# Smaller constant tables, a load plan by row length, pooling moved ahead of the attention pairs, and rotary tables moved into the MLP

## The chip, the cores and the metric

The kernel runs on one core of a Trainium2 chip. The metric is the device time of one execution in microseconds, the median of several runs. An engine is named as in the profile: PE (TensorE, matmuls), PEld (its weight loads), DVE (VectorE), ACT (ScalarE), POOL (GpSimd), SP (SyncE, which here issues all transfers that count).

## The reference

Two transformer blocks on 256 tokens of width 1024, in float32. Cut to what matters:

```python
def first_block(x, ...):
    h = rms_norm(x, g_mix_pre)
    u, q, k, v = split(h @ w_in)                     # 512 columns each
    y_pool = pool_mixer(u, w_pool, pool_scale)       # trailing means of 2, 4, 8, 16 tokens, per group
    y_attn = moba_attention(q, k, v, rel_bias)       # 8 heads, causal softmax with a position bias
    x = x + rms_norm(concatenate([y_pool, y_attn]) @ w_out, g_mix_post)
    x = x + rms_norm(conv_ffn(rms_norm(x, g_ffn_pre), w_up, conv_w, conv_b, w_down), g_ffn_post)
    return x + (p @ w_ple) * sigmoid(x @ w_ple_gate)

def second_block(x, mem, positions, ...):
    for i in range(2):                               # i = 0: sparse attention, i = 1: latent attention
        proj = x @ w_in[i]
        mix = nsa_mixer(proj, ...) if i == 0 else mla_mixer(proj, ...)   # both use rotary tables
        xa = memory_cross_attention(xq, mk, mv)      # mk, mv = mem @ mem_w_kv[i]
        x = layer_norm(ALPHA * x + concatenate([mix, xa]) @ w_out[i])
        x = layer_norm(ALPHA * x + hier_moe(x, ...)) # 16 experts, 2 per token, 3 matrices of 2 MB each
```

The rotary tables are cosines and sines of `positions` times fixed frequencies. The two sets of experts are 2 x 16 x 3 x 2 MB = 201 MB of the 293 MB that the kernel reads.

## The kernel before, in words

The kernel does not issue instructions as its functions are called. Each call is recorded as an operation (`Plan.record`), with what it reads and writes. At the end `Plan.order` goes through all operations as a list scheduler: for every engine it knows a modelled time at which the engine is free, and a model of each operation's duration (`Plan.cost`), and it places next the operation that can start first, in order of rank among those that can start about equally early. The rank is the place in the program; operations recorded inside `nc.filler()` get a rank behind everything, so they are taken only where an engine has nothing else to do, until something with an earlier rank needs them. The instructions are then emitted in this order. On the chip each engine takes its own instructions strictly in that order, and waits on semaphores; a modelled time decides nothing there but the order.

The model of a transfer: its issue takes 0.06 us of SP, and then all transfers share one modelled wire with 2.6e-6 us per byte. SP is not planned further than 3 us ahead of the wire.

Tiles are placed by the same scheduler: `arena` (208 units of 256 floats per partition, 1 KB each) for all working tiles, `tiny` (64 slots of 16 floats) for scalars per token such as means and inverse roots, and eight PSUM banks. A tile far ahead of the rest of the program may only be placed when enough room stays free; this is what stops loads that run ahead. A chunk of an expert's matrix is 256 x 512 floats, 512 KB, four arena units. Weights are float32; for the attention and MLP matrices they are split into a high and a low part on ACT, DVE and POOL (`split`, `put_split`: the cast to the high part, then a subtraction), and each product is three matmuls (`mm3`). Expert matrices are used in float32 as they are.

The order of the stages: `setup`, `block1` (projections `feat` and `tok512` of q, k, v; four pairs of heads, `pair(j)`, each with two query tiles, a softmax in `attend`, transposes and the product with v; then the projection of u and four `pool_mix(g)`; then the output projection, rows 512 to 1023 first: `order = [4, 5, 6, 7, 0, 1, 2, 3]`), the memory's keys and values for both layers (`memory`, as filler), the norms and transposes of the residual, `mlp` (eleven blocks of 256 hidden features, with `rope_tables` as filler at its start), `nsa`, `moe(0)`, `mla`, `moe(1)`, `finish`. Constant tables stay in SBUF the whole time: `ones` (128 x 128 floats), `busy` (128 x 512 bf16, the operand of dummy matmuls that PE runs in long gaps), `tiny`.

`row_bcast`, `rows_bcast` bring gains and biases of the norms to all partitions; `rows_bcast` picks a row by a matmul with a column `pick`, made anew for every row by one addition. `ln_gained` is the norm behind an expert stage; it writes into the tile `self.x`, whose old contents were last read at the fourth pair of experts (`pr == 3` in `moe`).

## Time and profile before

| | us |
|---|---|
| median of 3 runs | 1069.38 |
| lowest and highest | 1068.79, 1071.5 |
| the profiled execution | 1069.15 |
| its span, first to last instruction | 1067.5 |
| outside the span | 1.65 |

The granted clock of PE is 0.989 of full speed over the span. The page's first part gives the busy time of each engine. A stage's limit is not read from these shares but from windows cut at the stages, below. In a window row the columns are: the stretch, its length, then for PE, PEld, DVE, ACT and POOL the busy time with the number of instructions, then PE's granted clock, the mean busy share of the transfer engines, and GB/s.

### The profile page before, as it was taken

How to read it: one execution, taken by the hardware profiler on the slowest of the kernel's cores; microseconds unless marked ns; L12 is line 12 of the kernel's file. 1: busy time of each engine (PE TensorE's matmuls, PEld its weight loads, DVE VectorE, ACT ScalarE, POOL GpSimd, SP SyncE). 2: the span in 40 equal slices, each digit the busy share in tenths (PEclk: the TensorE clock that was granted, in tenths of full speed). 3: DMA queues.
4: the chain of work that ended last, by engine and by line, in shares of the span. 5: the costliest groups of instructions: out<-in, count | busy, mean ns of one | idle time of the engine just before them, and what ended most of it. 6: DMA issues, size and time to landing. Idle time of an engine off the chain costs nothing. (4 is left out here: it accounts for less than half of the span.)

```text
span 1067.5 us, 16507 instructions
## 1 busy us (share of the span) xinstructions
PE 1022.5 (96%) x6119; PEld 692.8 (65%) x6125; DVE 598.6 (56%) x1533; ACT 424.1 (40%) x973; POOL 78.7 (7%) x83
## 2 busy tenths in 40 slices
PE   8989899999999999999999899999999999999994
PEld 6878799999988888877444343435887434443431
DVE  6599999777767799996241111107996523111104
ACT  3475774343435456674231111107664422111103
POOL 0223200000002000310200000001100000000000
PEclk9999999999999999999999999999999999999998
DMA  8995115745576622387899999999669699999994
GB/s 304 360 307 200 58 44 195 242 155 184 210 271 198 217 100 79 100 311 261 281 382 386 385 369 377 382 387 375 245 228 322 229 360 386 386 387 387 387 387 151
DMA packets 172359, 292.85 MB, mean 274 GB/s; under 512 B 9251, under 2 KB 59340, under 8 KB 172268
## 3 DMA queue, kind: packets, MB, share of 16 engines
q1 hardware_dynamic: 172268, 291.69, 77.3%
q8 instruction: 51, 0.84, 0.3%
q14 instruction: 40, 0.33, 0.1%
HBM read 290.60 MB, written 1.06 MB: 273 GB/s over the span
## 5 line engine op out<-in xcount | busy, mean ns | idle before, releaser
L641 PE MATMUL ps<-span,span 128*128 128x256 f32 (+5 forms) x5464 | 954.2, 397 | 10.0 <-DVE span L641 7.0
L641 PEld LDWEIGHTS ps<-span,span 128*128 128x128 f32 (+3 forms) x5464 | 630.0, 173 | 304.4 <-issue 223.2
L641 DVE TENSOR_TENSOR span<-span,span 128x512 fp32r<-128x512 f32 (+7 forms) x425 | 256.7, 645 | 18.1 <-ACT span L641 15.4
L641 ACT CAST span<-span 128x512 fp32r<-128x512 f32 (+7 forms) x343 | 182.1, 581 | 55.2 <-DVE span L641 16.9
L641 DVE TENSOR_TENSOR span<-ps,span 128x512 fp32r<-128x512 f32 (+3 forms) x104 | 56.6, 549 | 149.5 <-ACT span L641 98.7
L641 DVE SCALAR_TENSOR_TENSOR span<-span,tiny,ps 128x512 f32<-128x512 f32 x16 | 12.0, 748 | 202.6 <-PE ps L641 191.3
L641 POOL TENSOR_TENSOR span<-span,span 128x512 fp32r<-128x512 f32 (+3 forms) x43 | 60.6, 1422 | 734.0 <-ACT span L641 443.9
L641 ACT CAST span<-ps 128x512 fp32r<-128x512 f32 (+1 forms) x63 | 32.3, 518 | 155.8 <-PE ps L641 145.4
L641 ACT COPY span<-ps 128x512 f32<-128x512 f32 (+1 forms) x106 | 50.8, 497 | 93.6 <-PE ps L641 87.1
L641 PE MATMUL ps<-cst,span 128*128 128x128 f32 (+1 forms) x363 | 59.5, 284 | 19.0 <-DVE span L641 12.4
L641 ACT ACTIVATE span<-ps 128x512 f32<-128x512 f32 (+3 forms) x33 | 18.5, 559 | 118.9 <-PE ps L641 113.2
L641 PEld LDWEIGHTS ps<-cst,span 128*128 128x128 f32 (+1 forms) x363 | 40.7, 142 | 36.2 <-DVE span L641 13.1
L641 ACT ACTIVATE span<-ps,tiny 128x256 f32<-128x256 f32 (+3 forms) x96 | 44.5, 473 | 21.5 <-DVE tiny L641 13.9
L641 ACT ACTIVATE span<-ps,vecs 128x256 f32<-128x256 f32 (+2 forms) x52 | 25.6, 524 | 67.3 <-PE ps L641 67.2
L641 ACT ACTIVATE span<-span 128x256 f32<-128x256 f32 (+4 forms) x36 | 16.1, 450 | 86.9 <-DVE span L641 86.5
L641 ACT ACTIVATE span<-span,tiny 128x256 f32<-128x256 f32 (+3 forms) x63 | 31.7, 525 | 11.9 <-DVE tiny L641 11.6
L641 DVE TENSOR_REDUCE tiny<-ps 64x1 f32<-64x2 f32 (+3 forms) x78 | 29.8, 391 | 9.2 <-PE ps L641 7.2
L641 DVE TENSOR_SCALAR span<-ps,vecs 128x256 f32<-128x256 f32 (+2 forms) x35 | 16.6, 491 | 29.4 <-ACT span L641 27.9
L641 DVE CAST span<-span 128x512 fp32r<-128x512 f32 (+6 forms) x76 | 28.5, 382 | 2.7 <-DMA span<-in_w_in_dram 1.8
L641 DVE SCALAR_TENSOR_TENSOR span<-span,vecs,span 128x255 f32<-128x255 f32 (+2 forms) x52 | 25.4, 498 | 0.8
L979 PE MATMUL ps<-busy 128*128 128x512 bf16 x88 | 23.3, 411 | 1.8 <-POOL busy L975 1.4
L641 DVE TENSOR_SCALAR span<-span,tiny 128x256 f32<-128x256 f32 (+2 forms) x73 | 22.7, 338 | 0.2
(107 smaller groups left out, 345.3 us busy)
## 6 DMA issues: line engine op xcount, KB each, us to landing
span<-in_moe_w_gate_dram SPq DMA_DIRECT2D x128, 512.0 KB, 8.9
span<-in_moe_w_up_dram SPq DMA_DIRECT2D x128, 512.0 KB, 9.2
span<-in_moe_w_down_dram SPq DMA_DIRECT2D x128, 512.0 KB, 8.7
span<-in_w_up_dram SPq DMA_DIRECT2D x22, 1024.0 KB, 5.3
span<-in_w_out_dram SPq DMA_DIRECT2D x12, 1024.0 KB, 10.5
span<-in_w_down_dram SPq DMA_DIRECT2D x11, 1024.0 KB, 5.0
span<-in_w_in_dram SPq DMA_DIRECT2D x7, 1024.0 KB, 13.0
span<-in_nsa_w_in_dram SPq DMA_DIRECT2D x7, 1024.0 KB, 9.9
```

Source lines behind the costliest of these rows:

```text
L641: getattr(eng, op)(*[real(x) for x in a], **{n: real(x) for n, x in k.items()})
L979: return lambda: nc.nc.tensor.matmul(nc.banks[bank], busy[:, :128], busy, start=True, stop=True)
```

## The change

Six things are changed together.

1. Tables that stay: `tiny` goes from 64 slots to 12 (and the free slots that far-ahead work must leave, from 12 to 4), `ones` from 128 columns to one that is read with stride zero, `busy` from 512 columns to 128 read four times. The arena goes from 208 to 212 units.
2. The plan's model of loads: an issue costs 0.47 us of SP instead of 0.06; a byte costs 2.584e-6 us where a row of the source is 2 KB or more, 2.8e-6 from 1 KB, 3.4e-6 below, and 4.6e-6 for what goes over the wire in the first 8 us.
3. In `block1` the projection of u and the load of `w_pool` come ahead of the pairs, `pool_mix(j)` comes ahead of `pair(j)`, and the output projection takes its rows in order.
4. `rope_tables` is recorded at the fifth block of the MLP (`c == 4`), still as filler, and may not start before the last operation recorded until then.
5. `ln_gained` writes into a new tile for x.
6. The columns `pick` are made once for all rows in the setup, and the rounded identity `identr` once in the setup instead of once in each `moe`.

```diff
-    FAR = {"ps": 2, "ws": 5, "row": 0, "tiny": 12}
+    FAR = {"ps": 2, "ws": 5, "row": 0, "tiny": 4}
...
-            return 1.0 if eng == "POOL" else 0.06
+            return 1.0 if eng == "POOL" else 0.47
...
+    @staticmethod
+    def pace(src, at):
+
+        step, n = src.ap[-1]
+        run = 4 * n if step == 1 else 4
+        return 4.6e-6 if at < 8.0 else 2.584e-6 if run >= 2048 else 2.8e-6 if run >= 1024 else 3.4e-6
...
-                wire = max(wire, end + 1.3) + o.bytes * 2.6e-6
+                wire = max(wire, end + 1.4)
+                wire += o.bytes * self.pace(calls[0][2][1], wire)
...
-ARENA = 208
-TINY = 64
+ARENA = 212
+TINY = 12
...
-            t, pick = nc.tile([D], F32, "row"), self.sml([1], F32R)
-            nc.vector.tensor_add(pick, self.ident[:, row:row + 1], self.ident[:, 32 + row:33 + row])
+            t, pick = nc.tile([D], F32, "row"), self.picks[:, row:row + 1]
...
-        self.ones = self.stay([128, 128], "ones")
+        self.ones = self.stay([128, 1], "ones")
...
-        busy = self.keep.tile([128, 512], BF, name="busy")
+        busy = self.keep.tile([128, 128], BF, name="busy")
...
+        self.identr, self.picks = self.stay([128, 128], "identr", F32R), self.stay([128, 8], "picks", F32R)
+        nc.scalar.copy(self.identr, self.ident)
+        nc.vector.tensor_add(self.picks, self.ident[:, 0:8], self.ident[:, 32:40])
...
         mixT = self.hilo()
+        self.feat(W, 0, 512, h, mul(u))
+        self.wp = self.mid([4, 128])
+        nc.sync.dma_start(self.wp, A["w_pool"].rearrange("g c d -> c g d"))
...
         for j in range(4):
+            self.pool_mix(j, u, mixT)
             pair(j)
-        self.feat(W, 0, 512, h, mul(u))
-        self.wp = self.mid([4, 128])
-        nc.sync.dma_start(self.wp, A["w_pool"].rearrange("g c d -> c g d"))
-        for g in range(4):
-            self.pool_mix(g, u, mixT)
...
-        order = [4, 5, 6, 7, 0, 1, 2, 3]
+        order = [0, 1, 2, 3, 4, 5, 6, 7]
...
-        with nc.filler():
-            self.rope_tables()
         Y = [[self.ps() for t in range(2)] for n in range(2)]
...
         for c in range(11):
+            if c == 4:
+                with nc.filler():
+                    nc.after = nc.ops[-1]
+                    self.rope_tables()
+                    nc.after = None
...
-        nc, x = self.nc, self.x
+        nc = self.nc
+        x = self.x = self.big([2, D])
...
-                idr = self.sml([128], F32R)
-                self.copy(idr, self.ident)
...
-                        self.returned(F[t][n], idr, z[0], z[1], False, False)
+                        self.returned(F[t][n], self.identr, z[0], z[1], False, False)
```

`finish` and `mla` read `self.x` instead of the name `x` that they took before; matmuls that used `ones` use it with stride zero.

## Rows read from the trace of the kernel before

**Rows 1.** The page: busy time of PE, share of the span, instructions.

```profile
PE 1022.5 (96%) x6119; PEld 692.8 (65%) x6125; DVE 598.6 (56%) x1533; ACT 424.1 (40%) x973; POOL 78.7 (7%) x83
```

**Rows 2.** Windows cut at the stages; columns as told above.

```profile
40.00:57.00 17.00, 16.21 (x134) 15.38 (x133) 5.82 (x12) 3.71 (x7) 6.31 (x5) 1.00 1.06 369
...
73.00:91.00 18.00, 18.00 (x98) 15.01 (x97) 17.98 (x42) 12.93 (x26) 3.77 (x10) 1.00 0.52 176
91.00:105.00 14.00, 14.00 (x79) 12.29 (x78) 14.00 (x30) 6.74 (x17) 7.27 (x4) 1.00 0.86 293
105.00:131.00 26.00, 19.83 (x144) 18.36 (x144) 24.75 (x85) 16.83 (x38) 6.44 (x5) 0.93 0.21 66
131.00:318.00 187.00, 187.00 (x1306) 175.71 (x1306) 148.43 (x317) 86.18 (x174) 2.63 (x2) 1.00 0.55 185
...
360.00:521.00 161.00, 155.36 (x1159) 126.39 (x1161) 136.25 (x454) 93.28 (x262) 16.93 (x20) 0.99 0.53 183
521.00:727.00 206.00, 200.48 (x942) 81.61 (x938) 33.56 (x63) 32.53 (x59) 3.43 (x4) 0.99 1.04 379
...
757.00:840.00 83.00, 79.53 (x539) 64.61 (x540) 70.92 (x199) 50.60 (x138) 6.61 (x5) 1.00 0.64 224
840.00:1050.00 210.00, 207.67 (x984) 83.84 (x980) 35.70 (x69) 35.25 (x63) 4.40 (x4) 1.00 1.04 378
```

**Rows 3.** Groups of PE, 131 to 318 us: shapes, count, busy us, mean ns, idle before.

```profile
L641 PE MATMUL ps<-span,span 128*128 128x256 f32 x1020 | 124.2, 283 | 0.0
L641 PE MATMUL ps<-span,span 128*128 128x512 f32 x284 | 66.5, 390 | 0.0
```

**Rows 4.** Timeline at 56 us: start, us, instruction, idle before and who ended it.

```profile
56.67 0.62 ACT L641 CAST span<-span 128x512 fp32r<-128x512 f32 x1 [12.32 <-DMA span<-in_memT_dram]
...
59.19 0.54 PE L641 MATMUL ps<-cst,span 128*128 128x128 f32 x2 [2.98 <-ACT span L641]
```

**Rows 5.** Timeline of PE, 105 to 131 us.

```profile
109.16 1.12 PE L641 MATMUL ps<-cst,span 128*128 128x128 f32 x4 [3.72 <-DVE span L641]
109.92 2.67 PE L641 MATMUL ps<-span,span 128*128 128x256 f32 x12
...
120.23 1.67 PE L641 MATMUL ps<-span,span 128*128 128x256 f32 x12
...
130.85 0.38 PE L641 MATMUL ps<-cst,r 128*128 128x128 f32 x1 [1.17 <-DVE r L641]
```

**Rows 6.** Groups of DVE by shape, 101.5 to 131 us.

```profile
L641 DVE SCALAR_TENSOR_TENSOR tiny<-tiny 128x1 f32<-128x1 f32 x24 | 7.3, 316 | 0.0
...
L641 DVE TENSOR_SCALAR span<-span 128x256 f32<-128x256 f32 x6 | 2.8, 463 | 0.0
L641 DVE SCALAR_TENSOR_TENSOR span<-span,span 128x256 f32<-128x256 f32 x4 | 2.7, 670 | 0.0
...
L641 DVE SCALAR_TENSOR_TENSOR span<-span 128x256 f32<-128x256 f32 x2 | 0.8, 418 | 0.0
```

**Rows 7.** Timeline of ACT, 126 to 140 us: table loads.

```profile
127.27 1.28 ACT L986 ACT_TABLE_LOAD   x1
128.56 0.20 ACT L986 ACTIVATE dump<-zero 128x1 f32<-128x1 f32 x1
...
135.31 1.28 ACT L986 ACT_TABLE_LOAD   x1
```

**Rows 8.** An issue in SP's timeline; two windows of 20 us for their GB/s.

```profile
4.71 0.47 SPq L641 DMA_DIRECT2D span<-in_w_in_dram  x1
...
20.00:40.00 20.00, 20.00 (x111) 16.42 (x110) 16.92 (x59) 12.24 (x23) 1.30 (x1) 1.00 1.09 356
...
560.00:580.00 20.00, 20.00 (x108) 9.13 (x106) 2.95 (x9) 3.12 (x6) 0.00 (x0) 1.00 1.05 386
```

**Rows 9.** The chain that ended last: start, us, what.

```profile
1021.18 10.79 DMA span<-in_moe_w_up_dram
```

**Rows 10.** Groups of DVE by shape, 20 to 24 us: the picks.

```profile
L641 DVE TENSOR_TENSOR span<-cst 128x1 fp32r<-128x1 f32 x8 | 1.1, 152 | 0.0
```

More of the change, by code (lines that the diff above doesn't have):

```diff
@@ L973, in setup @@
             nc.gpsimd.memset(self.eps[:, i:i + 1], e)
-        busy = self.keep.tile([128, 512], BF, name="busy")
+        busy = self.keep.tile([128, 128], BF, name="busy")
         nc.nc.gpsimd.memset(busy, 0.0)
         def idle(bank):
-            return lambda: nc.nc.tensor.matmul(nc.banks[bank], busy[:, :128], busy, start=True, stop=True)
+            return lambda: nc.nc.tensor.matmul(nc.banks[bank], busy, busy.unsqueeze(1).to_broadcast([128, 4, 128]), start=True, stop=True)
         nc.idle = idle
@@ L998, in setup2 @@
         nc.gpsimd.memset(self.ones, 1.0)
-        for t, s in ((self.identb, self.ident), (self.causalb, causal), (self.befb, before), (self.onesb, self.ones)):
+        self.identr, self.picks = self.stay([128, 128], "identr", F32R), self.stay([128, 8], "picks", F32R)
+        nc.scalar.copy(self.identr, self.ident)
+        nc.vector.tensor_add(self.picks, self.ident[:, 0:8], self.ident[:, 32:40])
+        for t, s in ((self.identb, self.ident), (self.causalb, causal), (self.befb, before), (self.onesb, self.ones.to_broadcast([128, 128]))):
             nc.vector.tensor_copy(t, s)
@@ L1014, in routers @@
             p = self.ps()
-            nc.tensor.matmul(p[:, :40], self.ones, s.rearrange("p a n -> p (a n)"), start=True, stop=True)
+            nc.tensor.matmul(p[:, :40], self.ones.to_broadcast([128, 128]), s.rearrange("p a n -> p (a n)"), start=True, stop=True)
             nc.vector.tensor_add(self.rb[:, l], self.rb[:, l], p[:, :20])
@@ L1853, in finish @@
     def finish(self, F, rows, out):
-        x = self.x
         def done(t, n):
             ns = slice(n * 512, n * 512 + 512)
-            self.nc.sync.dma_start(out[t * 128:t * 128 + 128, ns], x[:, t, ns])
+            self.nc.sync.dma_start(out[t * 128:t * 128 + 128, ns], self.x[:, t, ns])
         self.ln_gained(F, rows, done)
     def mla(self, F, rows):
-        nc, A, x = self.nc, self.A, self.x
+        nc, A = self.nc, self.A
         h = self.hilo()
         start = nc.ops[-1]
-        self.ln_gained(F, rows, lambda t, n: self.trans(x, t, n, h))
+        self.ln_gained(F, rows, lambda t, n: self.trans(self.x, t, n, h))
         W = A["mla_w_in"]
```

## Prediction, made before the changed kernel was run

> **What bounds the kernel now.** I began with the page: PE counts as busy for 96% of the span [rows 1], which says little, because a matmul that waits for its operands can count as busy. So I cut the span into stages [rows 2] and read three columns of each: PE, DVE and GB/s. Three kinds of stage appear.
>
> The first kind is the gated MLP, from 131 to 318 us. PE is busy for all of 187 us. Its two groups of matmuls, 1020 of 256 columns and 284 of 512 [rows 3], give 124.2 + 66.5 = 190.7 us (neighbours overlap a little), so this stage is PE work and nothing else. DVE has 38.6 us free there and ACT 100.8 us. What is added on those two engines can be hidden here; a stall of PE cannot.
>
> The second kind is the two expert stages, 521 to 727 and 840 to 1050 us: the transfers run at 379 and 378 GB/s [rows 2], and in an undisturbed window at 386 [rows 8]. They end when their bytes are in. The chain that ended last agrees: behind 1021 us it goes through a landing of an expert weight [rows 9]. Such a stage gets shorter only if more of its weights are already on the chip when it starts.
>
> The third kind is everything else, where DVE sets the pace: 17.98 of 18 us, 14.00 of 14, 24.75 of 26, and 136.25 of 161 in the sparse attention [rows 2]. In front of the MLP lie the places where PE truly stands still: 2.98 us at 56 us [rows 4], and a torn stretch from 105 to 131 us in which PE worked 19.83 of 26 us [rows 2, 5]. The stretch from 40 to 57 us is the odd one: DVE worked 5.82 of 17 us, while a cast on ACT stood 12.32 us in front of a transfer of the memory tokens [rows 2, 4]. Everything queued behind that cast on ACT, the exponentials of the first attention pair among it, had to wait as well.
>
> All times below are set against the profiled execution: 1069.15 us, of which the span is 1067.5. The median of the runs shown is 1069.38, 0.02% off, so no correction is made.
>
> **The change, part by part.**
>
> *The rotary tables go from the start of the MLP to its fifth block.* They are recorded as filler, taken when an engine has nothing earlier to do, and in the kernel before DVE takes them between 91 and 131 us, where it has nothing to spare. From 101.5 us on, where PE runs out of queued matmuls, three groups of their instructions are left: 2.8 + 2.7 + 0.8 = 6.3 us of DVE time [rows 6]. DVE is full there, and PE waits for it: 3.72 us in one place, 1.17 in another, and after the long one the granted clock of the stretch falls to 0.93 of full, so that twelve matmuls took 2.67 us that take 1.67 us a little later [rows 2, 5]. The most that can come back is PE's missing time: 26.00 - 19.83 = 6.2 us, and 1.0 us of slow clock, 7.2 us together. The least is nothing, if other filler moves into the freed time. I take 6.3 us, since the stretch is a chain through DVE: work taken out of it shortens it by its own length. In the MLP the tables meet 38.6 us of free DVE time and cost nothing; without that cover they would cost what they give here.
>
> The move has a price on ACT: the sine needs another table than the GELU. Before, the sine's load and the GELU's load stand one behind the other, ahead of the first GELU [rows 7]. In the middle of the MLP, it is GELU, sine, GELU: at least one load more, and three more if the two tables are not made together. A load took 1.28 us and the dummy behind it 0.20 us [rows 7], so 1.5 to 4.4 us of ACT's 100.8 free us: nothing, as long as two PSUM banks cover a GELU that is late.
>
> The Trainium skill speaks against this move: "ScalarE: Activation LUTs", What ACT_TABLE_LOAD costs, gives 1283 ns for the load and about 1380 ns for a drain, 2.66 us for every switch, and its rules say to do all of one set before switching. The load agrees with the 1.28 us of the row; the drain isn't seen there, since the dummy activation starts 0.01 us behind the load. By the page the extra switches would be 2.7 to 8.0 us of ACT time, an estimate, still less than what is free.
>
> *Pooling ahead of the attention pairs.* The projection of the pooled half (four tiles of 24 matmuls) is now recorded before the pairs, each group's pooling ahead of one pair, and the output projection starts with the pooled rows. So at 56 us PE has work that doesn't depend on a softmax: three tiles, 72 matmuls at 124.2 / 1020 = 0.12 us [rows 3], are 8.8 us, more than the 2.98 us hole. The hole could go entirely (-3.0), or come back behind the last pair, which now ends later (0, or worse: see the rivals). I take half, 1.5 us.
>
> *Loads planned by row length and issue time.* The list scheduler in the kernel now charges 0.47 us for an issue where it charged 0.06, and 2.8e-6 us a byte for rows of 1 KB where it charged 2.6e-6. Both are nearer to the trace: an issue took 0.47 us [rows 8], and 20 to 40 us, when weights with 1 KB rows load, went at 356 GB/s, that is 2.81e-6 [rows 8]. It moves no byte; it changes which instruction stands in front of which on ACT, DVE and PE. Its target is the cast that stood 12.32 us [rows 4]. DVE has 17 - 5.82 = 11.2 us unused there [rows 2]; the gain lies between nothing and these 11.2 us. I count nothing beyond the 1.5 us above, since PE itself was busy 16.21 of those 17 us [rows 2], and keep the upper end for the range.
>
> *Kept tables shrink; the arena grows from 208 to 212 units.* Four units of 1 KB per partition are one expert chunk of 512 KB. At 386 GB/s [rows 8] a chunk is 524288 / 386 = 1.36 us. Before each expert stage the loads run ahead until the arena is full: 757 to 840 us averages 224 GB/s, and 360 to 521 us 183 [rows 2]. So each of the two expert stages starts one chunk richer and ends 1.36 us earlier: 2 x 1.36 = 2.7 us. The lower end is nothing (the place isn't usable, or taken by something else), the upper end a second chunk each, 5.4 us.
>
> *The normalisation writes a fresh tile for x.* It frees eight units from the fourth pair of experts on, where loads already run at full rate; in the next attention stage x is alive again. Nothing. The wait that it removes (on the old x's readers) has long been over.
>
> *Small things.* Eight additions of 0.152 us become one, and the identity is converted once instead of twice [rows 10]; the conversions lay where DVE was busy 33.56 of 206 us [rows 2]. Below 1 us, at 21 us, where PE was busy anyway: nothing. The matrix of ones and the dummy's operand are read with stride zero: same columns, nothing.
>
> *The pool of small tiles falls from 64 slots to 12.* In the order in which the kernel before emits its work, at most nine are in use at once, so none should be short. If the two chains of the inverse root had to follow one another, it would cost half of the 7.3 us that DVE spends on their 24 steps [rows 6], 3.7 us; but in the trace they already follow one another. Nothing; 3.7 us for the range.
>
> **Sum:** 6.3 + 1.5 + 2.7 = 10.5 us. 1069.15 - 10.5 = 1058.65.
>
> **The rivals.** *Longer waits for the softmax (slower).* With the pooled projection gone ahead, the pairs have less to cover them. There are eight softmax steps (four pairs, two query tiles); the one uncovered step of the trace cost 2.98 us [rows 4]. All uncovered: 23.8 us. The cover left is the pooled half of the output projection, 48 matmuls of 66.5 / 284 = 0.234 us [rows 3], 11.2 us, since the memory's matmuls wait for a transfer that arrived at 56.67 us [rows 4]. 12.6 us would be new, against 6.3 and 2.7 gained: 1069.15 + 3.6 = 1072.8, slower by 0.34%. For it: DVE is full in the pairs. Against it: in the trace PE was covered from 59 to 105 us. It decides if the pairs start before the memory's transfer is in. Chance 0.12.
>
> *Other filler takes the freed DVE time.* The memory's splits are filler too, and in 101.5 to 131 us they are not used up. Then only the chunks are left: 1069.15 - 2.7 = 1066.5, within 0.3%. The same time comes out if the rescheduling costs in the sparse attention what it gives in front of the MLP. Chance 0.16.
>
> *The table loads show.* If the tables are made together and both loads fall on a GELU for which PE waits, 2 x 1.48 = 3.0 us come back: 1061.6. Against it: 100.8 us of free ACT time. Chance 0.07.
>
> *The better plan fills 40 to 57 us.* If ACT no longer stands in front of the memory's transfer, up to 11.2 us of DVE work moves forward, and the DVE-bound stretch behind it shortens by as much, limited by PE: I take the whole hole, 3.0, all of the 7.2 us, 2.7, and half of the 11.2 us: 18.5, so 1050.7. Chance 0.12.
>
> **How the numbers follow.** Forecast 0.53, softmax 0.12, filler 0.16, table loads 0.07, better plan 0.12. A measurement of this kernel tells 0.3%, 3.2 us, from no change. Faster: 0.53 + 0.07 + 0.12 = 0.72; same 0.16; slower 0.12. The range reaches below the better plan by the bound of the chunks (2.7) and a little of the unplaced half of the 11.2 us, to 1046, and above the filler case by the bound of the small tiles, 3.7 us, to 1070; outside lie the slower rival and the far ends, about 2 in 10.
>
> **What would show it.** Right: the three groups of [rows 6] named above gone from ahead of the MLP, the MLP's first matmul some 8 us earlier, the MLP still 187 us long with PE full, and each expert stage some 1.4 us less. Wrong: PE gaps behind ACT in the pairs; an MLP longer than 188 us with gaps at the table loads; a sparse attention (161 us) that is longer by what was won. If the time before the MLP doesn't shrink, the first and largest term is wrong.

## The result, and the profile of the changed kernel

The changed kernel takes 1055.87 us (median of 4 runs, 1053.94 to 1057.33), the kernel before 1069.62 beside it: a ratio of 0.9868, 95% interval 0.9847 to 0.9889. The forecast was 1058.65, so the sign, the range and the size held. The places did not all hold, and most of what follows is about that: 3.1 us less than forecast came ahead of the first choice of experts, 5.3 more in the two expert stages. That these differences partly cancel in the sum is luck.

The profiled execution took 1055.75 us, its span 1054.1. All stage times here are from one profiled execution of each kernel. Two marks cut them: the *choice*, at which DVE writes the experts' choice (`selb`), and the first statistics instruction of the norm behind an expert stage. From before to after, in us of the span (1067.5 - 1054.1 = 13.4):

| stretch | before | after | forecast | measured |
|---|---|---|---|---|
| start to the first choice | 504.0 | 499.3 | -7.8 | -4.7 |
| first expert stage | 222.6 | 218.1 | -1.4 | -4.5 |
| latent attention, to the second choice | 105.7 | 105.1 | 0 | -0.6 |
| second expert stage | 218.6 | 215.0 | -1.4 | -3.6 |
| the rest | 16.6 | 16.6 | 0 | 0 |

A stage's length from one profile is good to about 1 us: e9 below runs the instructions in the order of the changed kernel, and its stages differ from that kernel's by up to 1.1 us.

The page of after, busy time, answers to [rows 1]. PE is busy 4.9 us less and DVE the same; nothing in this line tells where 13.4 us went.

```profile
PE 1017.6 (97%) x6137; PEld 689.4 (65%) x6137; DVE 598.5 (57%) x1539; ACT 421.0 (40%) x964; POOL 67.7 (6%) x80
```

Windows of after at the stages, columns as in [rows 2]. The torn stretch ahead of the MLP is full (24.10 of 24.10 us of PE at a granted clock of 1.00, where it was 19.83 of 26 at 0.93), and DVE is as full as before (23.80). From 129.1 to 307.2 PE is full with the tables on board.

```profile
40.00:57.00 17.00, 17.00 (x136) 16.65 (x135) 8.25 (x15) 5.04 (x9) 1.54 (x1) 1.00 1.07 370
73.00:91.00 18.00, 17.89 (x110) 13.60 (x110) 17.78 (x44) 14.56 (x45) 5.77 (x5) 0.94 0.42 134
...
105.00:129.10 24.10, 24.10 (x197) 23.79 (x196) 23.80 (x85) 17.23 (x43) 3.90 (x3) 1.00 0.40 121
129.10:307.20 178.10, 178.10 (x1256) 167.85 (x1256) 141.96 (x312) 80.49 (x160) 1.59 (x1) 1.00 0.55 186
...
180.00:220.00 40.00, 40.00 (x275) 37.30 (x274) 39.88 (x91) 22.36 (x44) 1.59 (x1) 1.00 0.42 140
```

Groups of DVE in after, 101.5 to 129 us, against [rows 6]. The groups of 128x256 are gone, as forecast. But the splits (128x512 to fp32r) are now fourteen.

```profile
L649 DVE TENSOR_TENSOR span<-span,span 128x512 fp32r<-128x512 f32 x14 | 9.5, 684 | 0.0
L649 DVE SCALAR_TENSOR_TENSOR span<-ps,vecs,span 128x128 fp32r<-128x128 f32 x16 | 4.6, 341 | 0.0
L649 DVE SCALAR_TENSOR_TENSOR tiny<-tiny 128x1 f32<-128x1 f32 x24 | 4.2, 183 | 0.0
```

In the kernel before the same groups (101.5 to 131 us) had six of them:

```profile
L641 DVE TENSOR_TENSOR span<-span,span 128x512 fp32r<-128x512 f32 x6 | 5.1, 847 | 0.0
```

Timelines of after: the memory's cast still stands in front of its transfer [rows 4], PE's hole at 56 us is gone and one of 2.14 us is now at 71 us, and there are three table loads where [rows 7] had two. Behind the gap at 71 us the granted clock is 0.60 of full over 71 to 75 us. Before, it stayed at 1.00 behind the hole at 56 us (55 to 61 us) and was 0.61 behind the gap of 3.72 us (109 to 113 us).

```profile
57.95 2.18 ACT L649 CAST span<-span 128x512 fp32r<-128x512 f32 x4 [12.82 <-DMA span<-in_memT_dram]
...
71.10 0.77 PE L649 MATMUL ps<-cst,span 128*128 128x128 f32 x2 [2.14 <-ACT span L649]
...
130.31 1.28 ACT L993 ACT_TABLE_LOAD   x1
131.61 0.20 ACT L993 ACTIVATE dump<-zero 128x1 f32<-128x1 f32 x1
...
216.41 1.28 ACT L993 ACT_TABLE_LOAD   x1
...
223.38 1.28 ACT L993 ACT_TABLE_LOAD   x1
```

**The expert stages, in bytes.** Windows of before: the first and second 10 us behind each choice, and then to the end of the stage.

```profile
504.00:514.00 10.00, 9.97 (x60) 5.22 (x58) 8.02 (x28) 3.91 (x8) 0.00 (x0) 1.00 0.22 69
514.00:524.00 10.00, 10.00 (x52) 4.06 (x52) 0.65 (x3) 3.10 (x5) 4.96 (x4) 1.00 0.95 329
524.00:726.60 202.60, 197.08 (x925) 80.72 (x924) 33.17 (x62) 32.41 (x58) 1.92 (x2) 0.99 1.04 380
832.30:842.30 10.00, 9.30 (x56) 4.91 (x55) 7.85 (x28) 3.94 (x8) 0.00 (x0) 1.00 0.51 171
842.30:852.30 10.00, 10.00 (x54) 4.10 (x52) 0.65 (x3) 3.10 (x5) 1.20 (x1) 1.00 1.02 371
852.30:1050.90 198.60, 196.27 (x926) 79.78 (x924) 34.49 (x65) 32.15 (x58) 3.21 (x4) 1.00 1.03 378
```

The same of after:

```profile
499.30:509.30 10.00, 9.73 (x58) 5.10 (x57) 7.95 (x28) 3.94 (x8) 0.00 (x0) 1.00 0.49 169
509.30:519.30 10.00, 10.00 (x54) 4.10 (x52) 0.64 (x3) 3.10 (x5) 1.28 (x2) 1.00 1.03 384
519.30:717.40 198.10, 194.64 (x925) 79.91 (x924) 34.49 (x65) 33.10 (x59) 3.13 (x3) 0.98 1.04 381
822.50:832.50 10.00, 9.34 (x56) 4.94 (x55) 7.91 (x28) 3.90 (x8) 0.00 (x0) 1.00 0.51 161
832.50:842.50 10.00, 10.00 (x52) 4.06 (x52) 2.26 (x5) 3.11 (x5) 2.52 (x2) 1.00 0.67 224
842.50:1037.50 195.00, 193.20 (x926) 79.26 (x924) 33.09 (x63) 32.34 (x58) 1.90 (x2) 1.00 1.04 382
```

Length times GB/s gives what was moved between a choice and the end of its stage; it includes loads that run ahead for what follows. First stage: before 0.69 + 3.29 + 76.99 = 80.97 MB, after 1.69 + 3.84 + 75.48 = 81.01. No byte less. But at 386 GB/s [rows 8] the first two windows lost 20 - 3.98 / 0.386 = 9.7 us of transfer time before and 20 - 5.53 / 0.386 = 5.7 after. So in this pair of profiles the first stage is shorter by 4.0 us less of standing behind its choice, with no fewer bytes. Part of the standing had only moved: over the 30 us ahead of the choice the transfers ran slower after, 270 GB/s where it was 300, which is 2.3 us more lost there.

```profile
474.00:504.00 30.00, 29.48 (x176) 22.53 (x176) 19.44 (x50) 14.35 (x31) 0.61 (x1) 1.00 0.88 300
...
469.30:499.30 30.00, 28.49 (x171) 21.98 (x170) 19.47 (x49) 14.30 (x31) 0.64 (x1) 1.00 0.76 270
```

Second stage: before 1.71 + 3.71 + 75.07 = 80.49 MB, after 1.61 + 2.24 + 74.49 = 78.34. That is 2.15 MB, four chunks, 5.6 us; of them 4.0 us were lost again in the first two windows (6.0 us of standing before, 10.0 after), and the stretch behind ran at 382 instead of 378 GB/s (2.1 us). -5.6 + 4.0 - 2.1 = -3.7, measured -3.6. So over both stages the time lost behind the choices is the same before and after, 15.7 us: 9.7 + 6.0 and 5.7 + 10.0. Counted by SP's issues, 39 of a stage's 192 chunks had been issued when its experts were chosen before, in both stages; after it was 40 and 43.

What the transfers stood for is in SP's own waits (us in total, times, longest) and issues. Before, from 504 us on, over 21 us: SP waited 20.8 us in all for PE to read tiles whose room the next chunk needed. One of these waits was 12.2 us long and began ahead of the choice; the issue behind it fell at 510.57, 6.6 us after the choice.

```profile
SPq L641 <- PE ps L641: 20.8, 8, 12.2
...
510.57 0.37 SPq L641 DMA_DIRECT2D span<-in_moe_w_up_dram  x1
```

After, 499 to 520 us: the longest wait, 9.9 us, ended with DVE, and the issue falls at 502.26, 3.0 us behind the choice.

```profile
SPq L649 <- PE ps L649: 10.3, 10, 3.0
SPq L649 <- DVE span L649: 9.9, 1, 9.9
...
502.26 7.44 SPq L649 DMA_DIRECT2D span<-in_moe_w_down_dram  x8
```

The chain that ended last no longer goes through a landing at the end of the second expert stage [rows 9]. In after it is PE alone for 100.90 us up to 1030.62, so what one more chunk would have given there is not shown:

```profile
929.72 100.90 PE ps L649 x485
```

### The profile page after: what moved, and what is told of

It is laid out like the page before. It is cut to its first block, busy times and chain, and to the rows that moved or that the text cites. A ratio compares the mean times of both kernels' runs of the same rounds, so it can differ in the third digit from the quotient of the medians.

```text
span 1054.1 us, 16529 instructions
## 1 busy us (share of the span) xinstructions
PE 1017.6 (97%) x6137; PEld 689.4 (65%) x6137; DVE 598.5 (57%) x1539; ACT 421.0 (40%) x964; POOL 67.7 (6%) x80
## 5 line engine op out<-in xcount | busy, mean ns | idle before, releaser
L649 PE MATMUL ps<-span,span 128*128 128x256 f32 (+5 forms) x5432 | 939.3, 396 | 6.9 <-DVE span L649 4.6
L649 PEld LDWEIGHTS ps<-span,span 128*128 128x128 f32 (+2 forms) x5432 | 619.3, 172 | 294.2 <-issue 231.9
L649 DVE TENSOR_TENSOR span<-span,span 128x512 fp32r<-128x512 f32 (+7 forms) x431 | 261.2, 645 | 20.2 <-ACT span L649 17.2
L649 ACT CAST span<-span 128x512 fp32r<-128x512 f32 (+6 forms) x329 | 175.0, 581 | 53.1 <-DVE span L649 14.6
L649 POOL TENSOR_TENSOR span<-span,span 128x512 fp32r<-128x512 f32 (+3 forms) x37 | 48.7, 1323 | 743.3 <-ACT span L649 417.7
L649 ACT ACTIVATE span<-span,tiny 128x256 f32<-128x256 f32 (+3 forms) x62 | 31.2, 525 | 13.3 <-DVE tiny L649 12.2
L649 DVE CAST span<-span 128x512 fp32r<-128x512 f32 (+6 forms) x90 | 34.0, 385 | 3.3 <-DMA span<-in_w_in_dram 1.6
L986 PE MATMUL ps<-busy 128*128 128x512 bf16 x106 | 27.6, 407 | 1.1 <-POOL busy L982 1.1
## 6 DMA issues: line engine op xcount, KB each, us to landing
span<-in_w_out_dram SPq DMA_DIRECT2D x12, 1024.0 KB, 11.2
```

Source lines behind the costliest of these rows:

```text
L649: getattr(eng, op)(*[real(x) for x in a], **{n: real(x) for n, x in k.items()})
L986: return lambda: nc.nc.tensor.matmul(nc.banks[bank], busy, busy.unsqueeze(1).to_broadcast([128, 4, 128]), start=True, stop=True)
```

## The experiments

Every kernel was timed beside the kernel before, whose median was between 1069.09 and 1070.11 in these comparisons. The stage columns are from one profiled execution each, which can lie 2.5 us off the median: when the first choice falls, then the lengths of the first expert stage, of the latent attention and of the second expert stage.

| run | median us | ratio, 95% | choice | expert 1 | latent | expert 2 |
|---|---|---|---|---|---|---|
| before | 1069.62 | | 504.0 | 222.6 | 105.7 | 218.6 |
| after | 1055.87 | 0.9868 (0.9847 to 0.9889) | 499.3 | 218.1 | 105.1 | 215.0 |
| e1 | 1060.14 | 0.9920 (0.9897 to 0.9944) | 501.1 | 217.9 | 105.9 | 213.8 |
| e2 | 1067.56 | 0.9995 (0.9979 to 1.0011) | 508.8 | 215.4 | 106.1 | 216.5 |
| e3 | 1060.63 | 0.9920 (0.9903 to 0.9937) | 496.8 | 222.6 | 106.2 | 214.7 |
| e4 | 1065.10 | 0.9942 (0.9920 to 0.9964) | 506.3 | 216.8 | 106.2 | 216.6 |
| e5 | 1056.69 | 0.9873 (0.9848 to 0.9897) | 498.4 | 219.5 | 106.3 | 214.9 |
| e6 | 1066.96 | 0.9973 (0.9961 to 0.9985) | 503.1 | 223.1 | 105.9 | 219.1 |
| e7 | 1064.51 | 0.9952 (0.9935 to 0.9968) | 498.2 | 222.3 | 106.0 | 218.4 |
| e8 | 1071.36 | 1.0007 (0.9993 to 1.0020) | 509.8 | 218.6 | 105.7 | 218.9 |
| e9 | 1057.28 | 0.9875 (0.9856 to 0.9893) | 499.5 | 219.2 | 105.0 | 214.7 |
| e10 | 1059.95 | 0.9903 (0.9887 to 0.9920) | 496.4 | 224.6 | 106.3 | 214.2 |
| e11 | 1056.51 | 0.9876 (0.9859 to 0.9892) | 502.3 | 215.0 | 106.3 | 214.2 |
| e12 | 1061.44 | 0.9913 (0.9896 to 0.9931) | 499.4 | 222.9 | 105.8 | 215.8 |

### One part of the change undone: e1 to e4

**e1**, the old model of loads in the changed kernel:

```diff
-            return 1.0 if eng == "POOL" else 0.47
+            return 1.0 if eng == "POOL" else 0.06
...
-                wire = max(wire, end + 1.4)
-                wire += o.bytes * self.pace(calls[0][2][1], wire)
+                wire = max(wire, end + 1.3) + o.bytes * 2.6e-6
```

> The changed kernel with the load model of before (0.06 us an issue, 2.6e-6 us a byte) and everything else of the change. Theory A: the new load model costs at the start, because it puts the write of the position-bias table ahead of five loads on SP, which then waits from 4.20 to 8.05 us for DVE; without it the last spread ahead of the MLP (129.1 us after, 131.1 before) comes about 4 us earlier, at 125, and the first unbroken run of projection matmuls starts at about 15.8 us instead of 19.8; the time is about 1052. Rival B: the new load model is what makes the expert stages 8.1 us shorter; then they go back to 222.6 and 218.6 us (218.1 and 215.0 after) and the time is about 1060, whatever the start gives.

1060.14, 4.3 us more than the changed kernel. The expert stages are as short as with the new model (217.9, 213.8), so the model is not what shortened them, and theory A's sign is missing too: the last spread comes at 131.3 us, not at 125. The profiled execution shows 2.4 us of the loss: the choice falls 1.8 us later, the rest is spread (latent attention 0.8, the end 1.2, the experts 1.4 back).

**e2**, the rotary tables back at the start of the MLP:

```diff
+        with nc.filler():
+            self.rope_tables()
...
-            if c == 4:
-                with nc.filler():
-                    nc.after = nc.ops[-1]
-                    self.rope_tables()
-                    nc.after = None
```

> The changed kernel with the rotary tables back at the start of the MLP. Theory A: the tables cost DVE 6.3 us in the stretch before the MLP, so the last spread moves from 129.1 to about 135 us and the time is about 1062. Rival B: DVE's freed time went to other filler; the last spread stays within 2 us of 129.1 and the time within 2 us of 1055.9.

1067.56: 11.7 us of the 13.75 are gone, and what is left can't be told from nothing (its interval holds 1). The last spread comes at 133.3 us, 4.2 later. It is the largest part, and its loss sits ahead of the choice (+9.5 us), where the tables are. 11.7 is also more than the 6.3 that the prediction gave it.

**e3**, the projection of u and the pooling behind the pairs, the output projection in the old order:

```diff
-        self.feat(W, 0, 512, h, mul(u))
-        self.wp = self.mid([4, 128])
-        nc.sync.dma_start(self.wp, A["w_pool"].rearrange("g c d -> c g d"))
...
-            self.pool_mix(j, u, mixT)
             pair(j)
+        self.feat(W, 0, 512, h, mul(u))
+        self.wp = self.mid([4, 128])
+        nc.sync.dma_start(self.wp, A["w_pool"].rearrange("g c d -> c g d"))
+        for g in range(4):
+            self.pool_mix(g, u, mixT)
...
-        order = [0, 1, 2, 3, 4, 5, 6, 7]
+        order = [4, 5, 6, 7, 0, 1, 2, 3]
```

> The changed kernel with the pooling and its projection back behind the pairs, and the old order of the output projection. Theory A: moving it gave the 1.5 us of the prediction (half of the hole of 2.98 us): 1057. Rival B: it gave most of the 6 us by which the stretch from the first unbroken projection to the last spread got shorter (115.3 us before, 109.3 after): about 1060, and the stretch is 114 us or more.

1060.63, 4.8 us more. But not where the part lies: the choice falls 2.5 us *earlier* than in the changed kernel, and the first expert stage, 400 us behind the edit, is 4.5 us longer, as long as before. The time is rival B's, its sign is not there: the last spread comes at 126.6 us, 2.5 earlier.

**e4**, the arena at its old size in the changed kernel:

```diff
-ARENA = 212
+ARENA = 208
```

> The changed kernel with an arena of 208 units. Theory A: four units are one expert chunk for each expert stage, 2 x 1.36 us: 1058.6; the chunks issued when the experts are chosen go from 40 and 43 to 39 and 42. Rival B: the expert stages are shorter for another reason (the order of the loads); then their lengths stay 218.1 and 215.0 us within 1 us and the time is within 1.5 us of 1055.9.

1065.10, 9.2 us more, and again elsewhere than it was to be: 7.0 us ahead of the choice, 1.6 in the second expert stage, 2.1 in the rest, while the first is 1.3 us shorter. At the choices 40 and 42 chunks had been issued, where theory A had 39 and 42: taking four units away cost one chunk, in the second stage alone.

Undone one at a time, the four parts cost 4.3 + 11.7 + 4.8 + 9.2 = 30.0 us, and together they brought 13.75. Single removals can't be read as the parts' worth here.

### How much a new order alone moves: e5 and e6

Both change one figure of the scheduler's model, the hand-over between engines, by half a percent. No operation, byte or tile is added or removed; the order in which instructions are emitted comes out anew.

```diff
-    HOP = 0.2
+    HOP = 0.201
```

> The changed kernel, with the scheduler's margin between engines at 0.201 us instead of 0.200: no instruction is added or removed, only the order in which near ties fall (from the first 130 instructions on). Theory A: the order at near ties is worth little, the time stays within 2 us of 1055.9, and the differences of 4 to 12 us seen when single parts are undone are those parts. Rival B: any new order costs several us against the changed kernel, because this one's order happens to be a good one: 1059 to 1063, and then a part undone is only told from a new order where its own stage shows it.

> The kernel before with the same margin of 0.201 us. Theory A: within 2 us of 1069.1. Rival B: it moves by several us to either side; if it comes down to 1064 or below, part of the 13.3 us of the change is order alone.

The changed kernel so treated takes 1056.69 (+0.8), the kernel before 1066.96 against 1069.92 beside it (-3.0, its interval clear of 1). So in these two tries a new order alone was worth up to 3 us. That is as much as the arena's term of the forecast, and e1 and e3, 4.3 and 4.8 us, are little above it. The profiled execution of e6, 1069.47, was the slowest of its ten, so its stages don't show where the 3.0 us lie.

### One part alone, on the kernel before: e7, e8 and e12

**e7**, only the rotary tables moved (the diff of e2, reversed, on the kernel before):

> The kernel before with the rotary tables moved to the fifth block of the MLP and nothing else. Theory A: 6.3 us of DVE work less ahead of the MLP bring the last spread from 131.1 to about 126 and the time to 1063. Rival B: other filler takes the place: the last spread at 129 to 131, the time 1067 to 1069.

1064.51, 5.4 us less than the kernel before (3.4 to 7.0 by its interval): the 6.3 of the prediction is inside. The choice falls 5.7 us earlier, and both expert stages are unchanged. Its DVE groups, 101.5 to 128.7 us, repeat what after showed: the tables' groups gone, thirteen splits where there were six.

```profile
L641 DVE TENSOR_TENSOR span<-span,span 128x512 fp32r<-128x512 f32 x13 | 8.8, 684 | 0.8 <-ACT span L641 0.8
L641 DVE SCALAR_TENSOR_TENSOR tiny<-tiny 128x1 f32<-128x1 f32 x24 | 7.0, 298 | 0.0
```

So 6.3 us of tables left, and 8.8 - 5.1 = 3.7 us of splits came in. The last spread of the norm ahead of the MLP moved from 131.1 to 128.7, 2.4 us only. The other 3.4 came behind it: from the spread to the norm behind the MLP it is 179.6 us before and 178.2 in e7, from there to the choice 193.3 and 191.3. PE's matmuls of 256 columns show why. From 57 us to the spread, and from there to the norm behind the MLP, there are in the kernel before:

```profile
L641 PE MATMUL ps<-span,span 128*128 128x256 f32 x260 | 37.0, 295 | 0.6 <-DVE span L641 0.4
...
L641 PE MATMUL ps<-span,span 128*128 128x256 f32 x1008 | 122.7, 283 | 0.0
```

and in e7:

```profile
L641 PE MATMUL ps<-span,span 128*128 128x256 f32 x284 | 40.0, 299 | 0.0
...
L641 PE MATMUL ps<-span,span 128*128 128x256 f32 x996 | 121.2, 283 | 0.0
```

So 24 matmuls were drawn ahead of the spread, 12 out of the MLP and 12 from behind it (604 and 592 there). e6, the kernel before in another order, has the same 284 and 996 with the tables in their old place, and its last spread comes at 134.4. Against it e7's is 5.7 us earlier (one profile each): with the same work ahead of the spread, the stretch did get shorter by about the tables' length.

**e8**, only the smaller kept tables and the arena (the first part of the change) on the kernel before:

```diff
-ARENA = 208
-TINY = 64
+ARENA = 212
+TINY = 12
...
-        self.ones = self.stay([128, 128], "ones")
+        self.ones = self.stay([128, 1], "ones")
...
-        busy = self.keep.tile([128, 512], BF, name="busy")
+        busy = self.keep.tile([128, 128], BF, name="busy")
```

> The kernel before with the small tables and the arena of 212 units (and 12 small slots) and nothing else. Theory A: one chunk more for each expert stage, 2.7 us, the stages from 222.6 and 218.6 us to about 221.2 and 217.2, the time 1066.4. Rival B: the place shows in the expert stages more than once (the loads run ahead from an earlier point), stages of 218 and 215 us, the time about 1061. Rival C: nothing or slower, if the 12 small slots cost what the chunk gives.

1071.36, no gain. The first expert stage is 4.0 us shorter, the second not at all, and the choice falls 5.8 us later. Yet 40 and 41 chunks had been issued at its choices, one and two more than before. Its stages can't be set against those of before as they stand, since a stand of PE of 3 us lies in another stage (told under e10). The term of 2.7 us doesn't show in the time.

**e12**, both together on the kernel before (the diffs of e7 and e8):

> The kernel before with two parts of the change, the rotary tables at the fifth block of the MLP and the smaller kept tables with the arena of 212 units. These are the two terms that carried the forecast (6.3 and 2.7 us). Theory A, the two terms add and the rest of the change brings next to nothing: 1069.6 - 6.3 - 2.7 = 1060.6, with the MLP's last spread ahead of it about 6 us earlier than in the kernel before and both expert stages below 219 us. Theory B, each part brings what it brought alone (-5.3 for the tables, +1.0 for the arena, whose added room was paid for in front of the MLP): 1065.3, the second expert stage at 218 to 219 us. Theory C, the arena's loss in front was the order of that one run, and in another order its shorter expert stages come on top: at or below 1058, both expert stages at 215 to 218 us.

1061.44, 8.6 us less. As a sum that is theory A, and so is the last spread, at 125.1 us, 6.0 earlier. By the expert stages it is not: the first expert stage is as long as before (222.9, though it was 218.6 in e8, which lacks the stand told under e10), the second is short (215.8, though 218.9 in e8). Windows of e12 behind the two choices:

```profile
499.40:509.40 10.00, 9.99 (x60) 5.23 (x58) 7.92 (x28) 3.90 (x8) 0.00 (x0) 1.00 0.22 69
...
828.10:838.10 10.00, 9.29 (x56) 4.90 (x55) 7.85 (x28) 3.95 (x8) 0.00 (x0) 1.00 0.21 60
838.10:848.10 10.00, 10.00 (x54) 4.11 (x52) 0.64 (x3) 3.10 (x5) 0.00 (x0) 1.00 0.95 335
848.10:1043.90 195.80, 194.42 (x925) 79.22 (x924) 35.05 (x65) 32.28 (x58) 3.18 (x3) 1.00 1.04 380
```

The 69 GB/s behind the first choice are those of the kernel before. Behind the second, 0.60 + 3.35 + 74.40 = 78.35 MB were left, four chunks less than before, as in the changed kernel. So arena and tables together are enough for the second stage's four chunks, and the first stage got no shorter. Nor are all four the arena's: e4, with the arena of 208 units, had 42 issued, three more than before.

### What the rest is worth: e9, e10 and e11

**e9**, the norm behind the experts writes into the old x again:

```diff
-        nc = self.nc
-        x = self.x = self.big([2, D])
+        nc, x = self.nc, self.x
```

> The changed kernel with the normalisation behind the experts writing into the old tile for x again. The order of all instructions is the same as in the changed kernel; only places in the arena differ. Theory A (the prediction's): nothing, the expert stages stay 218 and 215 us, the time within 1.5 us of 1055.9. Rival B: the eight units that x holds from the fourth pair of experts on are what holds loads back; the second expert stage goes from 215.0 back to 218 or more and the time to 1059 or more.

1057.28, no stage differs by more than 1.1 us. The order of the instructions comes out the same, only places differ. The fresh tile is worth nothing that can be measured, as forecast.

**e10**, e3 with the hand-over of e5 (a second order for the same removal):

> The changed kernel with the pooling behind the pairs as in e3, and the margin of 0.201 us. In e3 the experts of the first layer were chosen at 496.8 us (499.3 in the changed kernel), but the first expert stage took 222.6 us (218.1). Theory A: the slow stage was that order alone, and pooling ahead of the pairs costs 2 to 3 us at the front: experts chosen at 496 to 498 us, a stage of 218, the time about 1053. Rival B: pooling behind the pairs brings the slow stage with it: 222 us again, the time about 1060.

1059.95 beside 1060.63 of e3: the 4 to 5 us that pooling behind the pairs costs survive a new order. So does their place: the choice is early (496.4), the first expert stage long (224.6).

The trace of e3 shows what is long in it. Some 100 us into the stage PE comes to the branch past the code for overfull experts (`overflow`). Its branch instruction there took 5.91 us, in the second stage 0.33, and PE stood for 5.99 us (6.01 in e10). The transfers fell to 291 GB/s in those 20 us. The changed kernel stood for 3.19 us at the same branch, at 371 GB/s. Of e3 (the branch's durations are in ns: least, median, most) and, behind the dots, of after:

```profile
L1840 PEldq COMPARE_BRANCH x2: 327/3120/5912, 596.9 to 922.0; - x2
603.01 11.05 PE L649 MATMUL ps<-span,span 128*128 128x256 f32 x44 [5.99 <-PEq L1840]
596.80:616.80 20.00, 14.01 (x61) 7.40 (x59) 2.47 (x4) 2.71 (x5) 0.00 (x0) 0.83 0.83 291
...
602.30 1.08 PE L649 MATMUL ps<-cst,span 128*128 128x128 f32 x4 [3.19 <-PEq L1839]
599.30:619.30 20.00, 17.00 (x79) 10.26 (x80) 2.86 (x5) 3.33 (x7) 0.00 (x0) 0.83 1.02 371
```

At 386 GB/s that is 4.9 us of transfer time lost in e3 and 0.8 in the changed kernel, so 4.1 of the 4.5 us. A stand of 2.9 to 3.2 us is there in before, e1, e5, e6, e7, e9 and e12 too, and none in e2, e4, e8 and e11; e2 and e8 have theirs, of 3.0 us, in the second stage. Why the branch is short in one kernel and long in another was not tested.

**e11**, the read-back of the position bias behind the first loads. In the changed kernel SP stands until 8.05 us in front of the write of that table, and the load behind it is issued at 8.39; here it is issued at 4.72:

```diff
-        rev = self.relative_bias()
+        tab = self.relative_bias()
...
+        nc.after = nc.ops[-1]
+        rev = self.back(tab)
+        nc.after = None
```

> The changed kernel with the write of the position-bias table recorded behind the eight loads that the first projection needs, so that SP doesn't stand from 4.20 to 8.05 us with six of those loads behind it. Theory A: the 97th projection matmul of 256 columns comes at 39.5 to 40 us, as with the old load model, instead of 42.0, and the time falls by about 2 us to 1053.8. Rival B: what is won at the start is lost before the MLP, where DVE sets the pace: the last spread stays within 1 us of 129.1 and the time within 1.5 us of 1055.9.

1056.51, no gain. The first projection starts at 11.4 instead of 12.6 us, and the choice falls 3.0 us *later*; the first expert stage is 3.1 us shorter. The last spread comes at 131.3 us, 2.2 later, so the earlier start was lost ahead of the MLP, by more than rival B had it. The first stage is the shortest of all, though its start is slow:

```profile
502.30:522.30 20.00, 19.97 (x111) 9.30 (x109) 8.57 (x31) 7.01 (x13) 4.96 (x4) 1.00 0.48 158
522.30:717.30 195.00, 193.23 (x925) 78.78 (x924) 33.22 (x63) 32.35 (x58) 1.91 (x2) 1.00 1.05 385
```

It lost 11.8 us behind its choice, but 44 chunks had been issued by then, and without a stand at the branch the rest ran at 385 GB/s.

## Why the prediction was right, and where its steps were not

**The sign and the size.** Faster by 13.75 us where 10.5 were forecast. Two of the forecast's signs of the mechanism are there: the three DVE groups of [rows 6] left the stretch, and the MLP carried them with PE full.

**The rotary tables, 6.3 us: right in size, in part in another place.** e7 measures 5.4 alone. The step that failed is to read "work taken out of it shortens it by its own length" as if nothing moved in, and with it the sign "the MLP's first matmul some 8 us earlier": it came 2.0 us earlier (131.1 to 129.1; 2.4 in e7). That mark moves with the order: in e6, with nothing moved, it came 3.3 us later, in e12 6.0 us earlier. The rival *other filler takes the freed DVE time* described what happened in that stretch, and drew the wrong end from it: the 24 matmuls that e7 drew ahead aren't lost, they are missing later. PE's own gaps did close: of the four in the torn stretch (3.72, 0.64, 0.38 and 1.17 us, the first and the last in [rows 5]) none is left in after. And the 6.3 us were not all work of the tables: 2.1 of them were waits for POOL, as the last section shows.

**MLP.** Forecast 187 us with PE full. From the last spread to the norm behind the MLP it is 179.6 us before and 178.1 after, PE full; e6 has 178.1 with the tables in their old place, so the 1.5 us are not the move's. From 180 to 220 us, where the tables now are, DVE is at 39.88 of 40 us: the cover held with 0.12 us to spare in that stretch. The rival of the table loads falls: one load more than before, no gap of PE at it; in e7 it is three more, with PE as full. The Trainium skill ("ScalarE: Activation LUTs", What ACT_TABLE_LOAD costs) adds a drain of about 1380 ns to each load; in after too the dummy starts 1.30 us behind the load's start, 0.02 us behind its end, and no drain is seen.

**Pooling, 1.5 us: its hole moved, not closed.** The hole of 2.98 us at 56 us is gone, one of 2.14 stands at 71 us. That is the forecast's "or come back", though between the pairs and not behind the last one: PE stands 0.84 us less where 1.5 were counted, and the slow clock that [rows 5] shows at 109 us is now here (0.94 over 73 to 91 us). The rival of eight uncovered softmax steps falls: this is PE's one gap behind ACT from 60 to 102 us. What e3 and e10 give pooling, 4 to 5 us, isn't ahead of the MLP but in the first expert stage, at the longer stand of PE at a branch. No step of the prediction leads there, and whether the place of the pooling causes the stand isn't shown.

**Load plan, 0 us (0 to 11.2).** The rival *better plan fills 40 to 57 us* falls: the cast stands 12.82 us as it stood 12.32, DVE has 8.25 us of work in those 17 instead of 5.82. Undone, it costs 4.3 us, in no one place; with an order's own effect at up to 3 us, a worth of its own isn't shown.

**Arena, 2.7 us: the term that was mis-sized.** The expert stages gave 8.1 us. "One chunk each" holds by the issues of the first stage (39 to 40), though it moved no fewer bytes behind its choice; in the second it was four, of which 4.0 us went again while the transfers stood. Nor is it the arena alone: e8, with the arena and not the rest, gained no time, and e4 has three of the four chunks without it. The step that failed is the rule that a stage begins with a full arena and then runs at full rate, and with it "gets shorter only if more of its weights are already on the chip". [rows 2] averaged over the stage and hid its first 20 us, in which 9.7 and 6.0 us of transfer time were lost before the change. It was in the trace, and I hadn't cut the window there. Together the two stages still lose the same 15.7 us.

**What stays open.** Which part shortens the first stage. In the profiles, all seven of the changed kernel's forms that keep pooling ahead of the pairs (after, e1, e2, e4, e5, e9, e11) have a first stage of 215.0 to 219.5 us, and all without it 222.3 to 224.6, except e8 at 218.6. But they get there in different ways. After, e2, e4 and e9 lose 5.7 to 7.9 us in the first 20 us behind the choice with 40 or 41 chunks issued; e1, e5 and e11 lose 10.5 to 11.8 with 43 or 44. In e3 and e10 the stand at the branch is longer, and the four without it (e2, e4, e8, e11) include the three shortest. So a quick start is not the common cause, and the link through 400 us of schedule wasn't shown.

**Small tiles.** No step of the inverse roots got slower: the 24 steps take 4.2 us instead of 7.3. The bound of 3.7 us wasn't needed. Why they got faster is told below.

## What to carry to other kernels

Cut a transfer-bound stage at its start before costing it: of some 20 us behind a dependence 9.7 and 6.0 were lost here, the change moved 4.0 us of that from one stage to the other, and a mean over the stage shows none of it. Look for stands at branches as well: here PE stood for 0, 3 or 6 us at one of them, in kernels whose edits lay elsewhere. In a kernel whose order comes from a list scheduler, time a null replan first (here up to 3 us), and read the parts by adding them alone as well as by removing them; 30 us of removals stood for 13.75. Filler that leaves a full engine can be replaced by other filler, and part of its gain then shows up later, not on the spot.

## What the runs showed of the hardware that I had not expected

In [rows 6] I read 316 ns as the price of a tiny step of the inverse root. It is a mean of two things. In the kernel before, three such steps of the two norms ahead of the MLP took 1.24 to 1.25 us where others took 0.14 to 0.22, each while POOL ran a subtraction of two SBUF tiles, and each ended within 0.03 us of it (here 127.56 + 1.25 = 128.81 against 127.33 + 1.47 = 128.80):

```profile
127.33 1.47 POOL L641 TENSOR_TENSOR span<-span,span 128x512 fp32r<-128x512 f32 x1 [5.06 <-DVE tiny L641]
127.56 1.25 DVE L641 SCALAR_TENSOR_TENSOR tiny<-tiny 128x1 f32<-128x1 f32 x1
129.07 0.21 DVE L641 SCALAR_TENSOR_TENSOR tiny<-tiny 128x1 f32<-128x1 f32 x1
```

Three larger instructions of the stretch were held too. One is a split of 128x512 that took 1.70 us where others took 0.68, while POOL was at work from 102.21 to 105.20 us. Two are of the rotary tables, 128x256, at 1.43 and 1.37 us where others took 0.41 and 0.28:

```profile
102.35 1.70 DVE L641 TENSOR_TENSOR span<-span,span 128x512 fp32r<-128x512 f32 x1
...
117.34 4.92 POOL L641 TENSOR_TENSOR span<-span,span 64x512 fp32r<-64x512 f32 x3 [12.14 <-ACT span L641]
119.69 1.43 DVE L641 SCALAR_TENSOR_TENSOR span<-span,span 128x256 f32<-128x256 f32 x1
121.05 1.37 DVE L641 TENSOR_SCALAR span<-span 128x256 f32<-128x256 f32 x1
```

So about 6.3 us of DVE's full stretch, 3.2 in the tiny steps and 3.1 in these, were waits for POOL that count as busy, and 2.1 of them stood in the 6.3 us that I read as the tables' work. In after one of the 24 steps began 0.006 us ahead of a POOL instruction and took 0.16 us, and none began during one: together they took 4.2 us. One TENSOR_TENSOR of tiny tiles, at 120.63 us, was held there and took 1.16 us. In e7 three steps again took over a microsecond, and the 24 still take 7.0 us. The Trainium skill says this of the two engines ("SBUF — State Buffer", Who interferes with whom): a DVE instruction with two SBUF inputs contends with a GpSimd instruction that reads SBUF, and the one that comes second waits for the whole of the other. The rows on the steps and the splits agree; the instruction at 121.05 has one tile as its input and was held as well, which this sentence doesn't cover. It makes POOL's splits dear exactly where a chain of DVE steps sets the pace, and it was visible before the change, as two durations of one shape.
